# A two-layer encoder trunk on one core: two of the sums of Winograd's seven products merged into one VectorE operation, the up block split ahead of the gate block, one more pair on seven products, and the first unit's copies dealt out

## The chip, the core and the metric

The kernel runs on one core of a Trainium2 chip. TensorE (PE) multiplies, VectorE (DVE) and ScalarE (ACT) work on the vectors, GpSimd (POOL) does a few of them, and SP issues most transfers. The metric is the device time of one execution in microseconds. Before the change it is 1954.49 us, the median of three runs that lie between 1954.39 and 1954.78. The profiled execution took 1953.67 us, of which 1951.9 us lie between its first and its last instruction.

## What is computed

The input is 256 tokens of width 2048 in float32, with BATCH 1. There are two layers. In the first the token mixer is grouped-query attention (16 query heads, 4 key heads, head size 128), in the second a gated linear recurrence with a short convolution. After each mixer stands the same feed-forward part, with a hidden width of 5632:

```python
x = x + mix
x = x + swiglu(rms_norm(x, norm_ffn[i]), ffn_w_gate[i], ffn_w_up[i], ffn_w_down[i])

def swiglu(h, w_gate, w_up, w_down):
    return (jax.nn.silu(h @ w_gate) * (h @ w_up)) @ w_down
```

The change lies wholly in the feed-forward part, and there in `h @ w_gate` and `h @ w_up`. The two feed-forward parts are the stretches from about 265 to 950 us and from about 1260 us to the end.

## The kernel before

**Precision.** TensorE is fed a float32 number as a sum of two numbers of a shorter type (fp32r): hi is the value cast by ScalarE, lo is the value less hi, subtracted by VectorE. A product of two blocks is then three matmuls: hi by hi, lo by hi and hi by lo (`product`, L322 to L328). Every weight therefore passes ScalarE once (a cast) and VectorE once (a subtraction) before TensorE can use it.

**A unit.** The hidden width is worked off in 11 units of 512 features a layer, numbered 0 to 10 (`unit`, L765). In a unit the contraction over 2048 goes in eight pairs of 256 rows, numbered 0 to 7. For one pair the weights are a 2 by 2 arrangement of blocks of 128 by 512: b11 and b21 are the two row halves of the gate weights, b12 and b22 those of the up weights. The tokens are a 2 by 2 arrangement as well, with two row halves of the pair and two halves of the 256 tokens. A plain pair makes all eight block products, 24 matmuls. A pair on seven products (a "seven" below) forms sums of weights and of tokens first, in Winograd's way, and makes seven products, 21 matmuls. `SEVEN` names the pairs that do so, and `FEWER` the shorter lists of units 0, 1 and 2.

**The weights of a seven** (`load_seven`, L155 to L196). Two transfers of 512 KB on SP's queue bring the gate weights into raw[0] and the up weights into raw[1], each 128 by 1024. Then

- t1, the sum of b11 and b12, is formed in place of b12, by VectorE where the three loads before were plain (L175), and otherwise by a transfer that accumulates, issued by GpSimd (L177);
- raw[0] and raw[1] are split into hi and lo, 1024 wide (cast L164, subtraction L165);
- t2, t3 and t4 are formed one after another by three additions or subtractions 512 wide (L170), each cast by ScalarE (L171), and each given its lo (L172).

A plain pair takes two loads of 1024, each with one cast (L146) and one subtraction (L147).

**Order.** TensorE's instructions stand as written. Those of the other engines are placed by a scheduler, but two chains bind it: every cast of a weight follows the cast before it ("cast"), and every subtraction or sum of weights the one before it ("rest"), by `behind`, L125. An engine executes its instructions in the order in which they stand. hi and lo live in a ring of seven tiles, raw in a ring of eight, and t2 has two tiles of its own.

**The end of a unit.** VectorE adds the accumulators (`sums` L779 to L784, then L802 and L805), ScalarE applies SiLU, VectorE multiplies (L806) and transposes 32 by 32 blocks (L409), and 16 copies of 32 by 256 (L417) put these blocks in place. The hidden features are then split (cast L812, subtraction L813). Where `beside` is set, the copies are dealt out: four stand at each of the next four sevens, at the `tail.pop(0)()` of `load_seven`. Otherwise all 16 stand together. From unit 2 on, two groups of the down projection follow a unit (96 matmuls on plain weights), whose sums ScalarE scales (L829) and GpSimd adds to x by an accumulating transfer.

Of the kernel before, what the change touches and what calls it, by code (L numbers as in the profile page):

```python
# [27 lines left out]
PARTS = [8, 8, 8, 8, 12]  # L28
UNIT = 4
SEVEN = (0, 1, 2, 4, 5, 6)  # L30
FEWER = {0: (0, 5, 6), 1: (4, 5, 6), 2: (1, 4, 5, 6)}
HALF = 8
CHUNK = HALF * P
WIDE = 512
# [41 lines left out]
def trunk(ctx, tc, w, out):  # L76
# [48 lines left out]
    def behind(key, i):  # L125
        if key in newest:
            follow(i, newest[key])
        newest[key] = i
        for rule in [rule for rule in ahead if key == rule[2]]:
            rule[0] -= 1  # L130
            if rule[0] == 0:
                follow(i, rule[1])
                ahead.remove(rule)
# [21 lines left out]
    def load_seven(srcs, soon):  # L155
        raw = [landing([P, 2, WIDE]) for _ in range(2)]
        for r, src in zip(raw, srcs):
            sync.dma_start(out=r, in_=src)
        (b11, b21), (t1, b22) = ([r[:, j, :] for j in range(2)] for r in raw)
        got = {}  # L160

        def two(src, names):
            hi, lo = parts([P, 2, WIDE])
            behind("cast", act.copy(hi, src))  # L164
            behind("rest", dve.tensor_tensor(lo, src, hi[:].bitcast(F32), ALU.subtract))  # L165
            for j, name in enumerate(names):
                got[name] = hi[:, j, :], lo[:, j, :]

        def combine(o, x, y, op, hi, lo):
            behind("rest", dve.tensor_tensor(o, x, y, op))  # L170
            behind("cast", act.copy(hi, o))  # L171
            return lambda: behind("rest", dve.tensor_tensor(lo, o, hi.bitcast(F32), ALU.subtract))  # L172

        if soon:
            behind("rest", dve.tensor_tensor(t1, b11, t1, ALU.add))  # L175
        else:
            pool.dma_start(out=t1, in_=b11, accum_op=ALU.add)  # L177
        two(raw[0], ("b11", "b21"))
        two(raw[1], ("t1", "b22"))
        if tail:  # L180
            tail.pop(0)()
        one = [tmp(t, (P, WIDE), F32R) for t in ("ohi", "olo")]
        hi, lo = parts([P, 2, WIDE])
        got["t2"] = tuple(one)
        got["t3"], got["t4"] = ((hi[:, j, :], lo[:, j, :]) for j in range(2))
        t2 = b22
        rests = [
            combine(t2, t1, b22, ALU.add, *got["t2"]),
            combine(b11, t2, b11, ALU.subtract, *got["t3"]),
            combine(b21, t2, b21, ALU.add, *got["t4"]),  # L190
        ]
        while parted:
            follow(parted.pop(), newest["cast"])
        for rest in rests:
            rest()
        return got  # L196


# [226 lines left out]
    class Norm:  # L425
# [38 lines left out]
        def form(self, c, src):  # L464
            v, t = (tmp("form", (P, 2 * S)).rearrange("p (a b) -> p a b", a=n) for n in (2, 4))
            for j in range(2):
                act.activation(v[:, j, :], src[:, j, :], AF.Copy, scale=col(self.g[0], self.g[1] + 2 * c + j))
            (a11, a21), (a12, a22) = ([v[:, j, a * P : (a + 1) * P] for a in range(2)] for j in range(2))
            for i, x, y, op in (
                (0, a21, a22, ALU.subtract), (1, a11, a21, ALU.subtract),  # L470
                (2, t[:, 0, :], a11, ALU.subtract), (3, a12, t[:, 2, :], ALU.add),
            ):
                pool.tensor_tensor(t[:, i, :], x, y, op)
            hi, lo = (tmp(f"f{n}", (P, 4, P), F32R, bufs=len(SEVEN)) for n in "hl")
            act.copy(hi, t)
            dve.tensor_tensor(lo, t, hi[:].bitcast(F32), ALU.subtract)
            self.forms[c] = [(hi[:, i, :], lo[:, i, :]) for i in range(4)]
# [283 lines left out]
    def ffn(norm, nxt):  # L761
# [3 lines left out]
        def unit(seven, beside, engines, soon):  # L765
# [20 lines left out]
            for c in range(KT // 2):  # L786
                if c not in seven:
                    for pair in ((c11, c21), (c12, c22)):
                        wide(pair, xs, 2 * c, KT, [fresh(o) for o in pair])
                        if pair[0] is c11 and c == seven[-1] + 1:  # L790
                            sums()
                    continue
                wt, end = half(), c == seven[-1]
                n1, n3, n2, n4 = norm.forms[c]
                a11, a12, a22 = block(xs, 2 * c, 0), block(xs, 2 * c + 1, 0), block(xs, 2 * c + 1, 1)
                for o, y, b in (
                    (m1, a11, "b11"), (c11, a12, "b21"), (p5, n1, "t1"), (c12, n4, "b22"),
                    (p6, n2, "t2"), (p7, n3, "t3"), (c21, a22, "t4"),
                ):
                    product(o, y, wt[b], fresh(o), end and any(o is m for m in (m1, p5, p7, p6)))  # L800
# [21 lines left out]
        ends = np.cumsum(PARTS) // UNIT  # L822
        for what, i in ffn_plan():
            if what == "unit":
                hid[int(np.searchsorted(ends, i, "right"))] += unit(FEWER.get(i, SEVEN), 0 < i < ends[-1] - 1, (act,) if i < ends[-1] - 1 else (act, dve), i < ends[0])
            else:
                for a, acc in enumerate(wide_project(hid[i[0]], PARTS[i[0]], bank)):
                    t = tmp("form", (P, WIDE))
# [224 lines left out]
```

## Time and profile before

| | before |
|---|---|
| runs, us | 1954.39 to 1954.78, median 1954.49 |
| profiled execution, us | 1953.67, span 1951.9 |
| TensorE, ScalarE, VectorE, GpSimd busy | 99%, 74%, 91%, 21% |
| granted TensorE clock | 1.000 |
| from one unit's sums to the next, units 3 to 10 | 61.2 us |

In the profile, L12 is line 12 of the kernel. A row of the groups names the line, the engine, the operation, out<-in by the program's names without buffer numbers, the shape and the count; then the busy time and the mean duration of one, and the idle time of the engine just before. In a timeline the columns are start, duration, engine, line and operation; square brackets hold the idle time before the instruction and who ended it. Where several equal instructions stand in one row, the duration is that of all. Matmuls are pipelined: each is shown with about 0.39 us, but they start 0.2267 us apart, as the starts in the timeline show.

### The profile page before, as it was taken

The page shows a single profiled execution, that of the slowest core. Times are in us where ns is not written, and L with a number is a line of the kernel's source. Part 1 is how long each engine was busy: PE and PEld are TensorE (multiplying, and loading weights), DVE is VectorE, ACT ScalarE, POOL GpSimd, SP SyncE. Part 2 cuts the span into 40 slices and gives each one's busy share as a digit, 9 for nine tenths or more (in the row PEclk, how much of TensorE's full clock was granted, in tenths as well). Part 3 has the DMA queues.
Part 4 walks back from the last instruction along what each step waited for, and adds up shares of the span by engine and source line. Part 5 has one row for each costly group of instructions (what it writes and reads, how often), then busy time and mean ns, then how long its engine had stood idle before and what let it go on. Part 6 is the DMA issues. An engine that isn't in the chain of part 4 may idle for free.

```text
span 1951.9 us, 27724 instructions
## 1 busy us (share of the span) xinstructions
PE 1939.2 (99%) x9264; PEld 1626.1 (83%) x9264; DVE 1771.2 (91%) x2425; ACT 1450.3 (74%) x2366; POOL 403.0 (21%) x497
## 2 busy tenths in 40 slices
PE   9999999999999999999999999999999999999999
PEld 8898888788888888888899998887888888888887
DVE  7878698999999999998799997898999999999993
ACT  7677686777777777777699887866778776787772
POOL 0443250011101111010466450520101110011100
PEclk9999999999999999999999999999999999999999
DMA  8434746697878978787365556565878888788872
GB/s 320 157 127 152 248 157 201 197 270 238 249 232 242 261 243 246 233 243 248 127 218 192 189 164 246 173 200 171 250 236 246 247 247 255 228 245 255 244 258 86
DMA packets 131729, 426.44 MB, mean 218 GB/s; under 512 B 14721, under 2 KB 14977, under 8 KB 131585
## 3 DMA queue, kind: packets, MB, share of 16 engines
q1 hardware_dynamic: 108944, 383.21, 58.2%
q0 software_dynamic: 22496, 41.43, 11.9%
q8 instruction: 73, 1.20, 0.2%
q14 instruction: 72, 0.58, 0.1%
q10 hardware_dynamic: 144, 0.02, 0.0%
HBM read 382.13 MB, written 2.10 MB: 197 GB/s over the span
## 4 chain that ended last, share of the span: by engine, by line
PE 92%; DVE 5%; issue 1%; ACT 1%; DMA 1%; POOL 0%; SPq 0%; ACTq 0%; DVEq 0%; POOLq 0%
PE acc L327 14%; PE acc L324 14%; PE acc L325 14%; PE pm L327 11%; PE pm L325 11%; PE pm L324 11%; PE acc L295 9%; PE acc L293 5%; PE pm L307 1%; PE pm L308 1%; PE pm L306 1%; DVE lo L147 1%; DVE lo L165 1%; ACT hi L146 0%; DVE raw L170 0%
## 5 line engine op out<-in xcount | busy, mean ns | idle before, releaser
L147 DVE TENSOR_TENSOR lo<-raw,hi 128x1024 fp32r<-128x1024 f32 (+1 forms) x474 | 577.8, 1247 | 75.3 <-ACT hi L146 73.7
L146 ACT CAST hi<-raw 128x1024 fp32r<-128x1024 f32 (+1 forms) x474 | 478.7, 1045 | 111.2 <-PE acc L325 68.3
L295 PE MATMUL acc<-xg,hi 128*128 128x512 f32 x896 | 293.3, 398 | 0.3 <-DVE xg L437 0.3
L165 DVE TENSOR_TENSOR lo<-raw,hi 128x1024 fp32r<-128x1024 f32 x232 | 275.3, 1217 | 7.4 <-ACT hi L164 5.3
L327 PE MATMUL acc<-lo,xg 128*128 128x512 f32 x712 | 277.9, 390 | 2.0 <-DVE lo L147 2.0
L325 PE MATMUL acc<-hi,xg 128*128 128x512 f32 x712 | 277.1, 389 | 0.0
L324 PE MATMUL acc<-hi,xg 128*128 128x512 f32 x712 | 277.1, 389 | 0.0
L164 ACT CAST hi<-raw 128x1024 fp32r<-128x1024 f32 x232 | 235.0, 1049 | 42.5 <-issue 14.9
L177 POOL DMA_DIRECT2D raw<-raw x90 | 77.8, 865 | 899.3 <-DVE raw L175 307.1
L293 PEld LDWEIGHTS acc<-xg,lo 128*128 128x128 f32 x896 | 168.1, 188 | 37.6 <-DVE lo L147 2.6
L327 PE MATMUL pm<-lo,act 128*128 128x512 f32 x512 | 199.2, 389 | 0.0
L325 PE MATMUL pm<-hi,act 128*128 128x512 f32 x512 | 199.2, 389 | 0.0
L324 PE MATMUL pm<-hi,act 128*128 128x512 f32 x512 | 199.2, 389 | 0.0
L417 ACT COPY two<-one 32x256 f32<-32x256 f32 x420 | 169.7, 404 | 24.7 <-DVE one L409 16.5
L293 PE MATMUL acc<-xg,lo 128*128 128x256 f32 x896 | 185.5, 281 | 1.0 <-DVE lo L147 1.0
L324 PE MATMUL acc<-hi,act 128*128 128x512 f32 x448 | 174.9, 390 | 0.4 <-DVE two L805 0.4
L327 PE MATMUL acc<-lo,act 128*128 128x512 f32 x448 | 174.4, 389 | 0.0
L325 PE MATMUL acc<-hi,act 128*128 128x512 f32 x448 | 174.4, 389 | 0.0
L171 ACT CAST hi<-raw 128x512 fp32r<-128x512 f32 x232 | 137.2, 622 | 32.7 <-DVE raw L170 31.3
L327 PEld LDWEIGHTS acc<-lo,xg 128*128 128x128 f32 x712 | 133.6, 188 | 32.7 <-DVE lo L147 5.3
L325 PEld LDWEIGHTS acc<-hi,xg 128*128 128x128 f32 x712 | 133.7, 188 | 28.0
L324 PEld LDWEIGHTS acc<-hi,xg 128*128 128x128 f32 x712 | 133.7, 188 | 27.4
(223 smaller groups left out, 3869.2 us busy)
## 6 DMA issues: line engine op xcount, KB each, us to landing
raw<-in_w_gate_dram SPq DMA_DIRECT2D x176, 512.0 KB, 4.7
raw<-in_w_up_dram SPq DMA_DIRECT2D x176, 512.0 KB, 5.4
raw<-in_w_down_dram SPq DMA_DIRECT2D x176, 512.0 KB, 4.5
raw<-in_w_in_dram SPq DMA_DIRECT2D x64, 512.0 KB, 4.4
raw<-raw POOLq DMA_DIRECT2D x90, 256.0 KB, 6.0
raw<-in_w_qv_dram SPq DMA_DIRECT2D x40, 512.0 KB, 4.2
raw<-in_w_o_dram SPq DMA_DIRECT2D x32, 512.0 KB, 3.7
x<-form POOLq DMA_DIRECT2D x64, 256.0 KB, 6.7
```

The costliest lines, as they stand in the source:

```text
L146: behind("cast", act.copy(hi[:, sl], raw[:, sl]))
L147: behind("rest", dve.tensor_tensor(lo[:, sl], raw[:, sl], hi[:, sl].bitcast(F32), ALU.subtract))
L164: behind("cast", act.copy(hi, src))
L165: behind("rest", dve.tensor_tensor(lo, src, hi[:].bitcast(F32), ALU.subtract))
L171: behind("cast", act.copy(hi, o))
L177: pool.dma_start(out=t1, in_=b11, accum_op=ALU.add)
L293: pe.matmul(acc[:, S:], w, xs[k][:, :S], start=False, stop=stop)
L295: pe.matmul(acc, w, xs[k], start=(k == 0), stop=stop)
L324: pe.matmul(o, xh, wh, start=start, stop=False)
L325: pe.matmul(o, xl, wh, start=False, stop=False)
L327: pe.matmul(o, xh, wl, start=False, stop=stop)
L417: m = (eng.copy if eng is act else eng.tensor_copy)(to[:, :, :, i, :], of[:, :, :, j, :])
```

## The change

Four things are changed; the signs of some sums of tokens change with the weights' and cost nothing else.

1. In `load_seven` the up block, with t1, is split first, then the gate block. t2 is now t1 less b22. The third and fourth sums are b11 less t2 and b21 less t2, so that one operation makes both: raw[0] less t2, where t2 is read twice by a broadcast. They are cast by one operation 1024 wide and get their lo by one subtraction 1024 wide.
2. TensorE takes the products in another order: t1 and b22 first, then b11 and b21, then t2, t3 and t4 as before.
3. Unit 1 makes pair 2 as a seven too, and unit 2 has pair 2 in the place of pair 1.
4. Unit 0's copies are dealt out to unit 1's sevens, as was done for the other units.

```diff
-FEWER = {0: (0, 5, 6), 1: (4, 5, 6), 2: (1, 4, 5, 6)}
+FEWER = {0: (0, 5, 6), 1: (2, 4, 5, 6), 2: (2, 4, 5, 6)}
...
-        def combine(o, x, y, op, hi, lo):
-            behind("rest", dve.tensor_tensor(o, x, y, op))
-            behind("cast", act.copy(hi, o))
-            return lambda: behind("rest", dve.tensor_tensor(lo, o, hi.bitcast(F32), ALU.subtract))
-
         if soon:
             behind("rest", dve.tensor_tensor(t1, b11, t1, ALU.add))
         else:
             pool.dma_start(out=t1, in_=b11, accum_op=ALU.add)
+        two(raw[1], ("t1", "b22"))
+        hi, lo = one = [tmp(t, (P, WIDE), F32R) for t in ("ohi", "olo")]
+        behind("rest", dve.tensor_tensor(b22, t1, b22, ALU.subtract))
         two(raw[0], ("b11", "b21"))
-        two(raw[1], ("t1", "b22"))
+        behind("cast", act.copy(hi, b22))
         if tail:
             tail.pop(0)()
-        one = [tmp(t, (P, WIDE), F32R) for t in ("ohi", "olo")]
-        hi, lo = parts([P, 2, WIDE])
-        got["t2"] = tuple(one)
-        got["t3"], got["t4"] = ((hi[:, j, :], lo[:, j, :]) for j in range(2))
-        t2 = b22
-        rests = [
-            combine(t2, t1, b22, ALU.add, *got["t2"]),
-            combine(b11, t2, b11, ALU.subtract, *got["t3"]),
-            combine(b21, t2, b21, ALU.add, *got["t4"]),
-        ]
+        t2 = b22.unsqueeze(1).to_broadcast([P, 2, WIDE])
+        behind("rest", dve.tensor_tensor(raw[0], raw[0], t2, ALU.subtract))
+        both = parts([P, 2, WIDE])
+        behind("cast", act.copy(both[0], raw[0]))
         while parted:
             follow(parted.pop(), newest["cast"])
-        for rest in rests:
-            rest()
+        behind("rest", dve.tensor_tensor(lo, b22, hi[:].bitcast(F32), ALU.subtract))
+        behind("rest", dve.tensor_tensor(both[1], raw[0], both[0][:].bitcast(F32), ALU.subtract))
...
-                    (m1, a11, "b11"), (c11, a12, "b21"), (p5, n1, "t1"), (c12, n4, "b22"),
+                    (p5, n1, "t1"), (c12, n4, "b22"), (m1, a11, "b11"), (c11, a12, "b21"),
                     (p6, n2, "t2"), (p7, n3, "t3"), (c21, a22, "t4"),
...
-                hid[int(np.searchsorted(ends, i, "right"))] += unit(FEWER.get(i, SEVEN), 0 < i < ends[-1] - 1, (act,) if i < ends[-1] - 1 else (act, dve), i < ends[0])
+                hid[int(np.searchsorted(ends, i, "right"))] += unit(FEWER.get(i, SEVEN), i < ends[-1] - 1, (act,) if i < ends[-1] - 1 else (act, dve), i < ends[0])
```

What the change moves is seen best engine by engine. In the rows below a name stands with its buffer number, as in raw_5332; the changed kernel's lines behind `load_seven` have numbers lower by six.

VectorE, pair 5 of unit 4 in the first layer, before. raw_5332 is the gate block, raw_5333 the up block with t1:

```order
L165 TENSOR_TENSOR lo_5338<-raw_5332,hi_5337 128x1024
L165 TENSOR_TENSOR lo_5342<-raw_5333,hi_5341 128x1024
L170 TENSOR_TENSOR raw_5333<-raw_5333 128x512
L170 TENSOR_TENSOR raw_5332<-raw_5333,raw_5332 128x512 x2
L172 TENSOR_TENSOR olo_5346<-raw_5333,ohi_5345 128x512
L172 TENSOR_TENSOR lo_5348<-raw_5332,hi_5347 128x512 x2
```

The same pair with the change, where raw_5280 is the gate block and raw_5281 the up block:

```order
L165 TENSOR_TENSOR lo_5286<-raw_5281,hi_5285 128x1024
L175 TENSOR_TENSOR raw_5281<-raw_5281 128x512
L165 TENSOR_TENSOR lo_5293<-raw_5280,hi_5292 128x1024
L181 TENSOR_TENSOR raw_5280<-raw_5280,raw_5281 128x1024
L186 TENSOR_TENSOR olo_5290<-raw_5281,ohi_5289 128x512
L187 TENSOR_TENSOR lo_5299<-raw_5280,hi_5298 128x1024
```

Eight instructions are six now, and only one of 512 stands between the sum L181 and the subtraction L187, which needs the cast of that sum; before, three stood between the last sum and the subtraction of its cast.

ScalarE in unit 4, pair 1, before. The copies L417 belong to the unit before, the L829 to the down projection:

```order
L164 CAST hi_5146<-raw_5141 128x1024
L164 CAST hi_5150<-raw_5142 128x1024
L417 COPY two_4532<-one_4918 32x8x32 x4
L829 ACTIVATE form_5074<-pm_5000,nr_3227 128x512
L829 ACTIVATE form_5077<-pm_5001,nr_3227 128x512
L171 CAST ohi_5158<-raw_5142 128x512
L171 CAST hi_5160<-raw_5141 128x512 x2
```

With the change:

```order
L164 CAST hi_5103<-raw_5099 128x1024
L164 CAST hi_5110<-raw_5098 128x1024
L823 ACTIVATE form_5034<-pm_4960,nr_3227 128x512
L823 ACTIVATE form_5037<-pm_4961,nr_3227 128x512
L177 CAST ohi_5107<-raw_5099 128x512
L411 COPY two_4510<-one_4878 32x8x32 x4
L183 CAST hi_5120<-raw_5098 128x1024
```

The four copies have moved from ahead of t2's cast to behind it, and stand now ahead of the cast of the third and fourth sums.

ScalarE at the first seven of unit 1 in the first layer, pair 4 before:

```order
L164 CAST hi_3801<-raw_3796 128x1024
L164 CAST hi_3805<-raw_3797 128x1024
L417 COPY two_3287<-one_3622 32x8x32 x16
L171 CAST ohi_3809<-raw_3797 128x512
L171 CAST hi_3811<-raw_3796 128x512 x2
```

With the change, where the first seven of unit 1 is pair 2:

```order
L164 CAST hi_3702<-raw_3698 128x1024
L164 CAST hi_3709<-raw_3697 128x1024
L177 CAST ohi_3706<-raw_3698 128x512
L411 COPY two_3287<-one_3613 32x8x32 x4
L183 CAST hi_3719<-raw_3697 128x1024
```

Sixteen copies in a row are four, behind t2's cast instead of ahead of it; the other twelve stand in the same place of the next three sevens.

More of the change, by code (lines that the diff above doesn't have):

```diff
@@ L177, in load_seven @@
             pool.dma_start(out=t1, in_=b11, accum_op=ALU.add)
+        two(raw[1], ("t1", "b22"))
+        hi, lo = one = [tmp(t, (P, WIDE), F32R) for t in ("ohi", "olo")]
+        behind("rest", dve.tensor_tensor(b22, t1, b22, ALU.subtract))
         two(raw[0], ("b11", "b21"))
-        two(raw[1], ("t1", "b22"))
+        behind("cast", act.copy(hi, b22))
         if tail:
             tail.pop(0)()
-        one = [tmp(t, (P, WIDE), F32R) for t in ("ohi", "olo")]
-        hi, lo = parts([P, 2, WIDE])
-        got["t2"] = tuple(one)
-        got["t3"], got["t4"] = ((hi[:, j, :], lo[:, j, :]) for j in range(2))
-        t2 = b22
-        rests = [
-            combine(t2, t1, b22, ALU.add, *got["t2"]),
-            combine(b11, t2, b11, ALU.subtract, *got["t3"]),
-            combine(b21, t2, b21, ALU.add, *got["t4"]),
-        ]
+        t2 = b22.unsqueeze(1).to_broadcast([P, 2, WIDE])
+        behind("rest", dve.tensor_tensor(raw[0], raw[0], t2, ALU.subtract))
+        both = parts([P, 2, WIDE])
+        behind("cast", act.copy(both[0], raw[0]))
         while parted:
             follow(parted.pop(), newest["cast"])
-        for rest in rests:
-            rest()
+        behind("rest", dve.tensor_tensor(lo, b22, hi[:].bitcast(F32), ALU.subtract))
+        behind("rest", dve.tensor_tensor(both[1], raw[0], both[0][:].bitcast(F32), ALU.subtract))
+        got["t2"] = tuple(one)
+        got["t3"], got["t4"] = (tuple(t[:, j, :] for t in both) for j in range(2))
         return got
@@ L469, in form @@
             for i, x, y, op in (
-                (0, a21, a22, ALU.subtract), (1, a11, a21, ALU.subtract),
-                (2, t[:, 0, :], a11, ALU.subtract), (3, a12, t[:, 2, :], ALU.add),
+                (0, a21, a22, ALU.add), (1, a21, a11, ALU.subtract),
+                (2, t[:, 0, :], a11, ALU.subtract), (3, a12, t[:, 2, :], ALU.subtract),
             ):
```

## The prediction

> **What bounds the kernel now.** I read the page's busy times first, then the windows, then the timelines of one unit.
>
> ```profile
> span 1951.9 us, 27724 instructions
> PE 1939.2 (99%) x9264; PEld 1626.1 (83%) x9264; DVE 1771.2 (91%) x2425; ACT 1450.3 (74%) x2366; POOL 403.0 (21%) x497
> ```
>
> TensorE is the bound, at 99%. A change of the vector engines' work helps only where TensorE waits. Where that is, the windows of 40 us show (columns: TensorE, weight loads, VectorE, ScalarE, GpSimd busy, with counts; then clock, DMA share, GB/s). A full window in the feed-forward part has 178 matmuls, as the first row has; the other four are those with fewer:
>
> ```profile
> 440.00:480.00 40.00, 40.00 (x178) 33.14 (x177) 38.49 (x48) 28.92 (x42) 4.37 (x5) 1.00 0.77 241
> 320.00:360.00 40.00, 39.17 (x171) 31.49 (x170) 35.47 (x45) 25.79 (x43) 0.86 (x1) 1.00 0.56 171
> 360.00:400.00 40.00, 38.61 (x167) 30.84 (x166) 38.72 (x49) 34.60 (x50) 1.71 (x2) 1.00 0.69 221
> 1320.00:1360.00 40.00, 37.96 (x164) 29.96 (x163) 34.98 (x46) 26.91 (x44) 0.00 (x0) 1.00 0.45 144
> 1360.00:1400.00 40.00, 39.52 (x172) 31.73 (x171) 38.56 (x47) 31.93 (x45) 1.71 (x2) 1.00 0.75 238
> ```
>
> 38 matmuls are missing in these four, at 0.2267 us 8.6 us. All four lie in units 1 and 2. In the first layer the loss begins here:
>
> ```profile
> 321.83 6.63 ACT L417 COPY two<-one 32x256 f32<-32x256 f32 x16 [1.10 <-DVE one L409]
> 329.14 0.69 DVE L172 TENSOR_TENSOR olo<-raw,ohi 128x512 fp32r<-128x512 f32 x1 [4.18 <-ACT ohi L171]
> 352.28 0.50 PE L327 MATMUL acc<-lo,xg 128*128 128x512 f32 x1 [0.82 <-DVE lo L147]
> 361.50 0.50 PE L324 MATMUL pm<-ohi,fh 128*128 128x512 f32 x1 [1.22 <-ACT ohi L171]
> ```
>
> Sixteen copies hold t2's cast, VectorE idles 4.18 us, and TensorE waits at the end of unit 1 and in the first seven of unit 2.
>
> Everywhere else TensorE is full, but VectorE nearly is too. These two windows are two whole units of the steady part (units 4 and 5):
>
> ```profile
> 452.00:513.20 61.20, 61.20 (x272) 50.67 (x271) 59.25 (x73) 45.62 (x67) 7.84 (x9) 1.00 0.83 244
> 513.20:574.40 61.20, 61.20 (x272) 50.68 (x271) 59.25 (x73) 45.73 (x67) 7.84 (x9) 1.00 0.84 246
> ```
>
> VectorE works 59.25 of 61.20 us. How near it is to being late shows at the unit's last seven, pair 6: t3's and t4's lo are done at 508.58 + 1.28 = 509.86 us, and TensorE takes t3's at 511.32.
>
> ```profile
> 508.58 1.28 DVE L172 TENSOR_TENSOR lo<-raw,hi 128x512 fp32r<-128x512 f32 x2
> 511.32 0.39 PE L327 MATMUL pm<-lo,fh 128*128 128x512 f32 x1
> ```
>
> So VectorE may become 1.46 us later per unit before TensorE waits. That number decides this change.
>
> **One seven before and after.** Pair 5 of unit 4, VectorE then ScalarE:
>
> ```profile
> 497.52 2.35 DVE L165 TENSOR_TENSOR lo<-raw,hi 128x1024 fp32r<-128x1024 f32 x2
> 499.90 0.69 DVE L170 TENSOR_TENSOR raw<-raw 128x512 f32<-128x512 f32 x1
> 500.63 1.29 DVE L170 TENSOR_TENSOR raw<-raw,raw 128x512 f32<-128x512 f32 x2
> 501.84 0.69 DVE L172 TENSOR_TENSOR olo<-raw,ohi 128x512 fp32r<-128x512 f32 x1
> 502.44 1.29 DVE L172 TENSOR_TENSOR lo<-raw,hi 128x512 fp32r<-128x512 f32 x2
> 503.65 2.36 DVE L165 TENSOR_TENSOR lo<-raw,hi 128x1024 fp32r<-128x1024 f32 x2
> 500.63 0.62 ACT L171 CAST ohi<-raw 128x512 fp32r<-128x512 f32 x1 [2.28 <-DVE raw L170]
> 501.41 1.17 ACT L171 CAST hi<-raw 128x512 fp32r<-128x512 f32 x2 [0.16 <-DVE raw L170]
> L806 DVE TENSOR_TENSOR two<-two,one 128x1024 f32<-128x1024 f32 x22 | 26.8, 1216 | 0.0
> L164 ACT CAST hi<-raw 128x1024 fp32r<-128x1024 f32 x232 | 235.0, 1049 | 42.5 <-issue 14.9
> L417 ACT COPY two<-one 32x256 f32<-32x256 f32 x420 | 169.7, 404 | 24.7 <-DVE one L409 16.5
> ```
>
> A seven takes 503.65 - 497.52 = 6.13 us of VectorE, without idle time: an operation of 1024 follows another after 1.14 us, one of 512 after 0.60, and one that needs the result just before it starts 0.03 after that has ended. Casts never hold it up, since two sums and two subtractions lie between a sum and the subtraction of its cast. ScalarE starts 0.04 to 0.09 after the sum.
>
> With the change VectorE goes: lo of the up block 1.14; t2, which overwrites what was just read, 0.03 + 0.69 = 0.72; lo of the gate block 1.14; the merged sum L181, dependent on what was just read, 0.03 + 1.22 = 1.25 (duration of L806, also f32 in place; no row has a repeated operand). Then ScalarE has to cast that sum, 1024 wide: start after 0.06, 1.05 long, and 0.03 later lo of both starts, 1.22 long. VectorE has only t2's lo (0.60) to do in between, and `behind` lets no later pair's work ahead. Sum: 1.14 + 0.72 + 1.14 + 1.25 + 0.06 + 1.05 + 0.03 + 1.22 = **6.61 us, 0.48 more**. Without the wait of some 0.6 us it would be 5.99, that is 0.14 less.
>
> The Trainium skill, in "Perfetto Trace Analysis", Optimizing Scalar/DVE Operations, says that grouping into larger operations can improve throughput if the engine is saturated, at about 60 ns of overhead for each DVE operation. The saving agrees with the rows (twice 0.60 less 1.14 is 0.06), but by that rule alone the change would be faster, the first rival's time. The same section says that where vector engines cause bubbles on others, breaking instructions up may let work be completed sooner; by that the merged cast comes too late, as in my sum.
>
> **A steady unit (3 to 10).** The rows for its pairs 1 to 6:
>
> ```profile
> 478.47 0.69 ACT L829 ACTIVATE form<-pm,nr 128x512 f32<-128x512 f32 x1 [0.67 <-PE pm L327]
> 479.06 0.61 ACT L171 CAST ohi<-raw 128x512 fp32r<-128x512 f32 x1
> 479.70 0.69 DVE L172 TENSOR_TENSOR olo<-raw,ohi 128x512 fp32r<-128x512 f32 x1 [0.91 <-ACT ohi L171]
> 480.31 1.29 DVE L172 TENSOR_TENSOR lo<-raw,hi 128x512 fp32r<-128x512 f32 x2
> 486.63 1.28 DVE L172 TENSOR_TENSOR lo<-raw,hi 128x512 fp32r<-128x512 f32 x2
> 490.10 2.35 DVE L165 TENSOR_TENSOR lo<-raw,hi 128x1024 fp32r<-128x1024 f32 x2
> 496.31 1.29 DVE L172 TENSOR_TENSOR lo<-raw,hi 128x512 fp32r<-128x512 f32 x2
> ```
>
> Pair 1 is tied to TensorE: the second scaling L829 waits for the down projection's last matmul and starts at 478.47 in either kernel, and t2's cast stands behind it. Before, pair 1 ended at 481.60. Now follow t2's cast (to 479.67), the four copies that the order put there (4 x 0.404, to 481.3), the cast of both (1.05) and lo of both (0.03 + 1.22): 483.6, **2.0 later**. Pair 2 took 6.31 (481.60 to 487.91) and takes 6.61: +0.30. The plain pair 3 stays. Pair 4 contains the hidden features' lo (L813): 490.18 to 497.60, 7.42. Now that subtraction fills the wait for the cast: 1.14 + 0.72 + 0.04 to t2's cast, 0.61, copies 1.62, cast L812 1.05, cast of both 1.05, and lo 1.22 with two starts, 7.5: +0.07. Pairs 5 and 6 +0.48 each. Together 3.33 us late against a margin of 1.46: TensorE waits **1.87 us in each steady unit**. The next unit starts from TensorE's scalings again, so each pays anew: 8 units in each of 2 layers, 29.9 us. ScalarE has room: a seven costs it 1.05 x 3 + 0.62 and 1.62 of copies, 5.4 of 6.6.
>
> **Units 0 to 2.** Dealing the copies out removes the 4.18 us of idle time. But unit 1's pair 2 takes VectorE 6.61 instead of 2 x 1.14 = 2.28, +4.33, and saves TensorE three matmuls, 0.68 (in two layers 1.36). Unit 0's sevens, in which small work fills the wait, I leave alone; its base copy stands behind one more cast, about 1 us, of which TensorE waits 0.3. Counted on so, unit 1's pair 2 ends with next to nothing in hand (0.1). Pair 3 gives 24 x 0.2267 = 5.44 less 2.28, +3.16. The three sevens each cost 6.61 against TensorE's 21 x 0.2267 = 4.76, -5.55, and L813 -0.9: TensorE waits 3.2. The wait behind the unit's sums stays (1.1, with the 0.82 quoted). Unit 2 now starts with two plain pairs, so the 1.22 there goes; its pair 2 ends about 0.75 ahead: 0.75 + 3.16 - 5.55 - 0.9, TensorE waits 2.5. Sum 0.3 + 3.2 + 1.1 + 2.5 = 7.1 a layer, 14.2 for 8.6 before: +5.6.
>
> **Sum.** 29.9 + 5.6 - 1.36 = +34.1 us on the profiled execution's 1953.67: 1987.8. That execution lies 0.8 below the runs' median, so the median forecast is **1988.6 us**.
>
> **Bounds.** L181 with a repeated operand: from 0.60 (a 512 row, if reading half as much counted) to 1.25; I take 1.25, as L806 handles the same 1024 outputs. If t2 and L181 pay no wait for the operation before them, a seven takes 6.38, and the units pay about 1.0 instead of 1.87: 1972. With 0.60 for L181 it takes 5.96 and no unit stalls, near the first rival's time. A start of the cast 0.16 after the sum instead of 0.06 adds 0.4 a unit: 1995.
>
> **Rivals.** *Fewer operations win.* If the wait for the cast is filled or short, VectorE saves 0.14 a seven and the 0.91 of pair 1, every wait of units 1 and 2 goes, and what is left is 1954.5 - 1.4 - 8.6 = 1944.5. For it: the 8.6 us are real, and the copies are dealt out. Against: VectorE's row order leaves one operation of 0.60 between L181 and L187. It decides if a seven costs less than about 6.0. *A draw.* The steady units absorb the delay, if it stays below 1.46 us a unit, and units 1 and 2 trade one wait for another: 1954 +- 4. *The accumulated t1 is late.* The up block is now split first, so ScalarE needs t1 a cast earlier:
>
> ```profile
> 487.94 0.33 SPq L158 DMA_DIRECT2D raw<-in_w_up_dram  x1
> 494.84 0.86 POOL L177 DMA_DIRECT2D raw<-raw  x1 [5.57 <-DVE act L813]
> raw<-raw POOLq DMA_DIRECT2D x90, 256.0 KB, 6.0
> ```
>
> From the freed buffer of pair 2 to t1 of pair 6 these are 6.9 + 6.0 = 12.9 us; from pair 2's end (490.2) to the need (505.4) there are 15.2. It decides when the two transfers take over 15.2; at 1.2 us late on three pairs a unit it costs 16 x 1.2 more: 2008.
>
> **Chances.** The forecast 0.74; draw 0.08, half of it still slower; fewer operations 0.10; late t1 0.08. The range 1966 to 2002 holds the forecast with its bounds and part of the third rival's. A measurement here can tell about 0.2%, 4 us, from no change: faster 0.10, same 0.04, slower 0.86.
>
> **What would show it.** Right: in the rows of the changed kernel, L187 waiting for L183 about 0.5 us in most of its 118 instances (some 50 us in all), a steady unit of about 63.1 us, and TensorE waiting at the last seven of each unit; no idle of 4 us in unit 1. Wrong: a steady unit of 61.2 us, or a pair's L165 following the pair before's by 6.1 us or less.

## The result and the profile after

The changed kernel takes 2004.67 us (median of four runs, 2003.53 to 2005.99) against 1954.61 for the kernel before: a ratio of 1.0257, with a 95% interval of 1.0244 to 1.0270. The forecast was 1988.6 in a range of 1966 to 2002. Direction and mechanism are as forecast; the size is 16 us short, and the time lies above the range. The profiled execution took 2003.53 us, 49.9 more than that of before.

The page's busy times of the changed kernel:

```profile
span 2001.7 us, 27361 instructions
PE 1964.3 (98%) x9258; PEld 1620.3 (81%) x9258; DVE 1768.2 (88%) x2199; ACT 1433.8 (72%) x2254; POOL 410.2 (20%) x501
```

VectorE has 226 instructions fewer and 3.0 us less work, ScalarE 16.5 us less. TensorE shows 25 us more although it has six matmuls fewer; it can't have more to do, so its busy time holds part of its delay (a matmul behind a wait is drawn with 0.50 us instead of 0.39, and the one ahead of it keeps its 0.39 although 0.2267 is its share). So busy times don't say what happened; the chain that ended last does. Its shares, of the changed kernel and then of the kernel before:

```profile
PE 63%; DVE 18%; ACT 9%; issue 7%; DMA 1%; POOL 1%; DVEq 0%; SPq 0%; ACTq 0%; POOLq 0%
```

```profile
PE 92%; DVE 5%; issue 1%; ACT 1%; DMA 1%; POOL 0%; SPq 0%; ACTq 0%; DVEq 0%; POOLq 0%
```

The chain now runs through VectorE and ScalarE. Where, the waits of the changed kernel tell (engine, line and what it waited for; us in total, times, longest):

```profile
DVE lo L187 <- ACT hi L183: 71.7, 96, 2.1
PE pm L321 <- DVE lo L187: 16.4, 39, 0.7
PE pm L321 <- DVE olo L186: 3.8, 19, 0.2
```

VectorE waits 71.7 us for the cast of the merged sum. TensorE waits for the lo of the merged sum ("lo of both" below, L187) and, less, for t2's lo (L186). Pairs 5 and 6 of unit 4 in the changed kernel, VectorE:

```profile
506.45 1.22 DVE L165 TENSOR_TENSOR lo<-raw,hi 128x1024 fp32r<-128x1024 f32 x1
507.70 0.69 DVE L175 TENSOR_TENSOR raw<-raw 128x512 f32<-128x512 f32 x1
508.31 1.22 DVE L165 TENSOR_TENSOR lo<-raw,hi 128x1024 fp32r<-128x1024 f32 x1
509.57 1.23 DVE L181 TENSOR_TENSOR raw<-raw,raw 128x1024 f32<-128x1024 f32 x1
510.71 0.69 DVE L186 TENSOR_TENSOR olo<-raw,ohi 128x512 fp32r<-128x512 f32 x1
511.97 1.23 DVE L187 TENSOR_TENSOR lo<-raw,hi 128x1024 fp32r<-128x1024 f32 x1 [0.57 <-ACT hi L183]
513.11 1.22 DVE L165 TENSOR_TENSOR lo<-raw,hi 128x1024 fp32r<-128x1024 f32 x1
518.57 1.23 DVE L187 TENSOR_TENSOR lo<-raw,hi 128x1024 fp32r<-128x1024 f32 x1 [0.51 <-ACT hi L183]
```

From one pair's L187 to the next these are 6.60 us, where a seven took 6.13; 0.51 is the wait. And TensorE at the end of that unit:

```profile
513.25 0.50 PE L321 MATMUL pm<-lo,fh 128*128 128x512 f32 x1 [0.21 <-DVE lo L187]
518.11 0.49 PE L321 MATMUL pm<-olo,fh 128*128 128x512 f32 x1 [0.20 <-DVE olo L186]
519.85 0.50 PE L321 MATMUL pm<-lo,fh 128*128 128x512 f32 x1 [0.53 <-DVE lo L187]
520.18 0.40 PE L318 MATMUL acc<-hi,xg 128*128 128x512 f32 x1
```

Three waits stand where the kernel before had none, and the matmul after a wait starts 0.33 us behind it (519.85 to 520.18), not 0.2267. The losses add up from the start of each unit's first matmul in both profiles, since the matmuls between two such starts are the same in number but for the three that unit 1 saves:

| stage, both layers together | forecast, us | measured, us |
|---|---|---|
| units 3 to 10 (16 units) | +29.9 (1.87 each) | +38.6 (2.34 in most) |
| units 0 to 2, with six matmuls fewer | +4.2 | +9.9 (4.35 and 5.60) |
| behind unit 10's sums | 0 | +1.5 |
| all else (attention, recurrence, start) | 0 | -0.1 |

### The profile page after: what moved, and what is told of

Same layout as the page of the kernel before. It is cut to its first block, busy times and chain, and to the rows that moved or that the text cites. A ratio compares the mean times of both kernels' runs of the same rounds, so it can differ in the third digit from the quotient of the medians.

```text
span 2001.7 us, 27361 instructions
## 1 busy us (share of the span) xinstructions
PE 1964.3 (98%) x9258; PEld 1620.3 (81%) x9258; DVE 1768.2 (88%) x2199; ACT 1433.8 (72%) x2254; POOL 410.2 (20%) x501
## 4 chain that ended last, share of the span: by engine, by line
PE 63%; DVE 18%; ACT 9%; issue 7%; DMA 1%; POOL 1%; DVEq 0%; SPq 0%; ACTq 0%; POOLq 0%
PE acc L318 9%; PE acc L321 9%; PE acc L319 9%; PE acc L289 9%; DVE lo L165 7%; PE pm L321 7%; PE pm L319 6%; PE pm L318 6%; PE acc L287 4%; ACT hi L183 3%; DVE raw L181 3%; DVE lo L147 3%; ACT two L411 2%; DVE lo L187 2%; PE pm L301 1%
## 5 line engine op out<-in xcount | busy, mean ns | idle before, releaser
L147 DVE TENSOR_TENSOR lo<-raw,hi 128x1024 fp32r<-128x1024 f32 (+1 forms) x470 | 573.6, 1248 | 73.0 <-ACT hi L146 71.7
L165 DVE TENSOR_TENSOR lo<-raw,hi 128x1024 fp32r<-128x1024 f32 x236 | 288.6, 1223 | 2.1 <-ACT hi L164 1.6
L321 PE MATMUL acc<-lo,xg 128*128 128x512 f32 x700 | 273.8, 391 | 2.9 <-DVE lo L147 2.9
L318 PE MATMUL acc<-hi,xg 128*128 128x512 f32 x700 | 273.8, 391 | 1.0 <-DVE one L796 1.0
L319 PE MATMUL acc<-hi,xg 128*128 128x512 f32 x700 | 273.2, 390 | 0.0
L164 ACT CAST hi<-raw 128x1024 fp32r<-128x1024 f32 x236 | 235.7, 1047 | 26.7 <-DVE raw L170 16.9
L187 DVE TENSOR_TENSOR lo<-raw,hi 128x1024 fp32r<-128x1024 f32 x118 | 144.6, 1225 | 71.8 <-ACT hi L183 71.7
L183 ACT CAST hi<-raw 128x1024 fp32r<-128x1024 f32 x118 | 123.9, 1050 | 69.2 <-DVE raw L181 67.7
L177 ACT CAST ohi<-raw 128x512 fp32r<-128x512 f32 x118 | 73.2, 620 | 134.9 <-DVE raw L175 117.6
```

What stands on the lines that cost most here:

```text
L147: behind("rest", dve.tensor_tensor(lo[:, sl], raw[:, sl], hi[:, sl].bitcast(F32), ALU.subtract))
L183: behind("cast", act.copy(both[0], raw[0]))
L187: behind("rest", dve.tensor_tensor(both[1], raw[0], both[0][:].bitcast(F32), ALU.subtract))
L318: pe.matmul(o, xh, wh, start=start, stop=False)
L319: pe.matmul(o, xl, wh, start=False, stop=False)
L321: pe.matmul(o, xh, wl, start=False, stop=stop)
```

## The experiments

All kernels but new_split_old_units have the new lists of sevens and unit 0's copies dealt out. "Lost per steady unit" is the median, over units 3 to 9 of both layers, of a unit's length by the matmuls' starts less 61.20, the kernel before's.

| kernel | median, us | ratio to before (95%) | lost per steady unit, us |
|---|---|---|---|
| changed | 2004.67 | 1.0244 to 1.0270 | 2.34 |
| new_split_old_units | 2006.71 | 1.0251 to 1.0284 | 2.39 |
| old_split_new_units | 1954.39 | 0.9992 to 1.0011 | 0.00 |
| t2_lo_first | 2037.70 | 1.0408 to 1.0445 | 3.96 |
| copies_ahead | 1992.65 | 1.0178 to 1.0214 | 1.39 |
| halves | 1994.45 | 1.0188 to 1.0220 | 1.87 |
| both_mended | 1978.24 | 1.0107 to 1.0139 | 0.90 |
| sums_apart | 1978.1 | 1.0099 to 1.0135 | 0.95 (in its profile) |
| apart_copies_ahead | 1953.10 | 0.9984 to 1.0003 | 0.00 |
| merged_gate_first | 1983.68 | 1.0134 to 1.0164 | 1.15 |
| skewed | 2008.64 | 1.0262 to 1.0295 | 3.22 |
| skewed_sevens | 2028.81 | 1.0363 to 1.0397 | 4.09 |
| skewed_gate | 1958.40 | 1.0011 to 1.0029 | 0.00 |
| skewed_gate_all | 1955.66 | 0.9996 to 1.0014 | 0.00 |

**The two halves of the change apart.** First load_seven and the order of products alone:

```diff
-FEWER = {0: (0, 5, 6), 1: (2, 4, 5, 6), 2: (2, 4, 5, 6)}
+FEWER = {0: (0, 5, 6), 1: (4, 5, 6), 2: (1, 4, 5, 6)}
...
-unit(FEWER.get(i, SEVEN), i < ends[-1] - 1,
+unit(FEWER.get(i, SEVEN), 0 < i < ends[-1] - 1,
```

> The change's load_seven and order of products (parts 1 and 2) with the lists of sevens and the bunched copies of before. Theory (the wait for the merged cast makes each seven longer): the steady units stay at 63.5 us from sums to sums, as in the changed kernel, 2.34 x 16 = 37 us; units 0 to 2 and the stall after unit 10 add a few us: 1992 to 2000. Rival (dealing out unit 0's copies and the new lists cost much of the 50 us, by what they push into the later units): steady units below 62.3 us and a time under 1980.

Measured 2006.71, above the expected 1992 to 2000; the steady units lose 2.39 us, as in the changed kernel (2.34), and units 0 to 2 lose 13.6 where the changed kernel loses 9.9. Then the lists and the dealt-out copies alone, on the kernel before:

> The new lists of sevens and the dealt-out copies (parts 3 and 4) with load_seven and the order of products of before. Theory: sevens stay at 6.13 us and steady units at 61.2; counted as in the prediction with 6.13 in the place of 6.61, units 0 to 2 lose some 3 us a layer where they lost 4, and six matmuls fewer save 1.36: 1951, between 1946 and 1953. Rival (the units' part costs something of its own): 1958 or more, since the changed kernel's early units lose 19 us in both layers.

Measured 1954.39, no change, against a forecast of 1951 (1946 to 1953). Its profile shows 2.7 us gained in units 0 to 2 (1.36 of it the six matmuls), and 4.6 lost in the recurrence between the layers, most of it at one place:

```profile
1008.21 0.47 PE L295 MATMUL acc<-xg,hi 128*128 128x512 f32 x1 [2.15 <-DVE act L382]
```

This wait makes 2.5 us. Behind it the granted TensorE clock was 0.50 (1010 to 1012 us; 0.79 and 0.85 in the 2 us before and after), and that makes 1.6 more. The edit doesn't touch this code, but the scheduler set other engines' work there in another order. That profiled execution was the longest of ten: the four with a mean clock of 1.000 took 1953.49 to 1954.12 us, the six with 0.998 or 0.999 1953.72 to 1955.64. How much of the wait itself the others have is left open. What is settled: parts 3 and 4 cost next to nothing and cannot be the 50 us; these come with parts 1 and 2.

**More of the wait.** t2's lo is moved ahead of the merged sum, so that nothing fills the wait for its cast:

```diff
+        behind("rest", dve.tensor_tensor(lo, b22, hi[:].bitcast(F32), ALU.subtract))
         t2 = b22.unsqueeze(1).to_broadcast([P, 2, WIDE])
         behind("rest", dve.tensor_tensor(raw[0], raw[0], t2, ALU.subtract))
...
-        behind("rest", dve.tensor_tensor(lo, b22, hi[:].bitcast(F32), ALU.subtract))
         behind("rest", dve.tensor_tensor(both[1], raw[0], both[0][:].bitcast(F32), ALU.subtract))
```

> The changed kernel, but t2's lo stands ahead of the merged sum, so that nothing is left between that sum and the subtraction that needs its cast. Theory (the wait for the cast of the merged sum sets the length of a seven): the wait grows by the 0.60 us that t2's lo no longer fills, pairs 2, 5 and 6 go from 6.6 to 7.2 us, and a steady unit, where pair 1 is held by ScalarE's copies anyway, loses 1.8 to 2.4 more: 16 x 2.1 = 34 us and some 8 in units 0 to 2, about 2045 (2030 to 2055). Rival (the amount of work counts, not its order): the same work, 2005.

Measured 2037.7, in the expected range, with a steady unit 1.6 us longer than in the changed kernel (1.8 to 2.4 expected): the work is the same, the order makes 33 us. The wait of the seven that ends at 520 us is 1.17 where it was 0.57:

```profile
517.55 1.22 DVE L182 TENSOR_TENSOR raw<-raw,raw 128x1024 f32<-128x1024 f32 x1
519.94 1.23 DVE L187 TENSOR_TENSOR lo<-raw,hi 128x1024 fp32r<-128x1024 f32 x1 [1.17 <-ACT hi L184]
```

**The copies' place.** The copies stand ahead of t2's cast again:

```diff
-        behind("cast", act.copy(hi, b22))
         if tail:
             tail.pop(0)()
+        behind("cast", act.copy(hi, b22))
```

> The changed kernel, but the four copies stand ahead of t2's cast again, as before the change. Theory (of pair 1's 2.06 us, 1.62 are the copies between t2's cast and the merged cast): pair 1 is only some 0.45 late, but the hidden features' lo no longer fills the wait of pair 4, +0.3 there; a steady unit is 3.6 - 1.6 + 0.3 = 2.3 late against 1.46 of margin, so it loses 0.8 to 1.0 where it lost 2.3: about 1980 (1972 to 1985). Rival (the copies' place does not matter, only the six waits): 2000 or more.

Measured 1992.65, above the expected 1972 to 1985: a unit still loses 1.39. In units 4 and 5 of this kernel VectorE waits for the merged cast in all six sevens of a unit, pair 4 included (0.54 us each), and for nothing else. Its 58.95 us of work a unit, these waits and the short starts behind an operation's own input fill the 62.7 us of the unit, so no margin is left that could swallow a delay.

**The merged cast and lo in halves**, the merged sum kept:

```diff
-        behind("cast", act.copy(both[0], raw[0]))
+        for j in range(2):
+            behind("cast", act.copy(both[0][:, j, :], raw[0][:, j, :]))
...
-        behind("rest", dve.tensor_tensor(both[1], raw[0], both[0][:].bitcast(F32), ALU.subtract))
+        for j in range(2):
+            behind("rest", dve.tensor_tensor(both[1][:, j, :], raw[0][:, j, :], both[0][:, j, :].bitcast(F32), ALU.subtract))
```

> The changed kernel, but the merged sum is cast and given its lo in two halves of 512 (the sum itself stays one operation of 1024). Theory (what costs is that VectorE waits for a cast of 1024): t3's cast of 0.62 ends while t2's lo of 0.60 runs, so the wait in a seven falls from 0.6 to about 0.1 and a seven to 6.2 us; pair 1, whose copies still stand behind t2's cast, stays 1.6 late, so a steady unit loses some 0.3 and the time is about 1960 (1953 to 1968). Rival (the other order of the two blocks costs, not the wait): 1995 or more.

Measured 1994.45, against the 1960 of the theory and close to the rival's 1995. The rival falls further down, with sums_apart and the copies ahead. The wait inside a seven did fall, but a seven became hardly shorter (pair 5 takes 505.49 to 512.05 us, that is 6.56). Pair 5 of unit 4 in this kernel, VectorE and then ScalarE:

```profile
508.61 1.23 DVE L181 TENSOR_TENSOR raw<-raw,raw 128x1024 f32<-128x1024 f32 x1
509.75 0.69 DVE L187 TENSOR_TENSOR olo<-raw,ohi 128x512 fp32r<-128x512 f32 x1
510.57 1.29 DVE L189 TENSOR_TENSOR lo<-raw,hi 128x512 fp32r<-128x512 f32 x2
512.05 1.23 DVE L165 TENSOR_TENSOR lo<-raw,hi 128x1024 fp32r<-128x1024 f32 x1 [0.18 <-ACT hi L164]
```

```profile
509.92 1.14 ACT L184 CAST hi<-raw 128x512 fp32r<-128x512 f32 x2 [1.83 <-DVE raw L181]
510.97 2.00 ACT L164 CAST hi<-raw 128x1024 fp32r<-128x1024 f32 x2
```

VectorE now waits 0.18 us for the cast of the next pair's first block, which stands behind the two casts of this one. ScalarE had been idle for 1.83 us, until the merged sum was done. So the cycle is: merged sum, 1.05 us of casts for it, one more cast of about 1 us for the next block, and only then can VectorE's next pair begin. The theory had looked for the wait inside the seven alone. With both edits:

> The changed kernel with the merged sum's cast and lo in two halves, and the copies ahead of t2's cast. Halves alone took a steady unit's loss from 2.34 to 1.87 us, the copies alone to 1.39. Theory A (the delays of the pairs add up against one margin): 1.39 - 0.47 = 0.9 is left, and units 0 to 2 as with the copies ahead, 1985. Theory B (pair by pair: pair 1 level, pair 2 +0.25, pair 4 +0.3, pairs 5 and 6 +0.43 each, 1.4 against a margin of 1.46): hardly any loss in the steady units, 1960 to 1970.

Measured 1978.24, and 0.90 us lost in a steady unit: theory A to the digit, though the whole is 7 us better, by units 0 to 2.

**No merging.** Two sums of 512, with their casts and lo as in halves; the up block still comes first:

```diff
-        t2 = b22.unsqueeze(1).to_broadcast([P, 2, WIDE])
-        behind("rest", dve.tensor_tensor(raw[0], raw[0], t2, ALU.subtract))
+        for b in (b11, b21):
+            behind("rest", dve.tensor_tensor(b, b, b22, ALU.subtract))
```

> The changed kernel (up block first, copies behind t2's cast), but the third and fourth sums are two operations of 512 again, each with a cast and a lo of 512. It takes away the merging and leaves the other order of the blocks. Theory (merging is what makes VectorE and ScalarE wait for each other): a seven takes 6.12 us, only pair 1 stays late, by the copies, 1.6 against 1.46, and a steady unit loses 0.1 to 0.4: about 1961 (1954 to 1968). Rival (the order of the blocks costs by itself, since the third sum now waits for the gate block): a steady unit loses 1.5 or more, 1985 to 1995.

> The same kernel as sums_apart (two sums of 512, up block first, copies behind t2's cast), for a profile of it. If only the merged cast made sevens longer, pairs 5 and 6 take 6.1 to 6.2 us here and the units' loss, about 1 us by the time of 1978, is that of pair 1 alone; if the order of the blocks lengthens a seven too, pairs 5 and 6 take 6.4 us or more.

Measured 1978.1, between the theory and its rival; the profile (1977.05) has pair 5 at 6.13 us again. Late is pair 1 above all, and there by ScalarE's copies. ScalarE, then VectorE:

```profile
481.59 0.69 ACT L825 ACTIVATE form<-pm,nr 128x512 f32<-128x512 f32 x1 [0.67 <-PE pm L323]
482.17 0.61 ACT L177 CAST ohi<-raw 128x512 fp32r<-128x512 f32 x1
482.81 1.65 ACT L413 COPY two<-one 32x256 f32<-32x256 f32 x4
484.49 1.14 ACT L184 CAST hi<-raw 128x512 fp32r<-128x512 f32 x2
```

```profile
485.14 1.29 DVE L189 TENSOR_TENSOR lo<-raw,hi 128x512 fp32r<-128x512 f32 x2 [1.43 <-ACT hi L184]
```

Pair 1 ends 486.43 - 481.59 = 4.84 us after the second scaling starts, which was 3.13 before: 1.71 late; pairs 2 and 3 add 0.47, pair 4 0.22, pairs 5 and 6 nothing. 2.40 less the margin of 1.46 is 0.94, and the loss is 0.95. That agreement is luck in part: 1.46 is the margin of a lo of both in one, while here TensorE takes t3's lo without a wait, waits ahead of it for t2's lo (0.27 us), and starts the plain pair's first lo behind it 0.15 us late. Taking the copies away from there as well leaves only the order of the blocks:

> sums_apart, and the four copies ahead of t2's cast again: of the change's load_seven only the order of the two blocks is left, with the new units. Theory (the copies between t2's cast and the next casts are what is left of the loss in sums_apart): the 0.9 us a unit that moving them gained in the other two kernels comes off again, 16 x 0.9 = 15, so 1978 - 15 = 1963 (1957 to 1967). Rival (up block first costs by itself): 1970 or more.

Measured 1953.10, below the expected 1957 to 1967 and level with the kernel before: 25 us for one line's place, and up block first costs nothing in this form. The table of both places, with the three forms of the sums (us lost per steady unit):

| | copies ahead of t2's cast | behind it |
|---|---|---|
| sums, casts and lo apart | 0.00 | 0.95 |
| sum merged, casts and lo apart | 0.90 | 1.87 |
| all merged, as in the change | 1.39 | 2.34 |

Each row loses 0.95 to 0.97 more from left to right, each column 0.90 to 0.92 more by the merged sum and 0.47 to 0.49 by the merged cast and lo. The steady losses add up to within 0.02. One common margin would not make them do so: it should swallow 1.46 us of whichever delay comes first. In the kernels with the copies ahead the second scaling no longer waits for TensorE (in copies_ahead both scalings stand without idle time). In copies_ahead, where VectorE waits for ScalarE alone, the two run in a cycle of their own:

```profile
486.59 1.27 ACT L823 ACTIVATE form<-pm,nr 128x512 f32<-128x512 f32 x2
```

Why the losses add up so exactly stays open. Merging with the old order of blocks:

> The changed kernel's merged sum, cast and lo, but the gate block is split first, as before the change, with the products in that order and the copies ahead of t2's cast; the units are the new ones. Theory (merging alone costs): a seven takes the same 6.6 us by the same sum, so it loses as the kernel with the copies ahead did, 1.4 us a unit: 1985 to 1997. Rival (up block first is half of the loss): a steady unit loses 0.7 or less, under 1975.

Measured 1983.68, just under the theory's 1985 to 1997, and 1.15 us lost in a unit: merging costs in either order, 9 us less with the gate block first than in copies_ahead.

**Merging with the wait filled.** load_seven is cut in two, and the next pair's up block is cast and subtracted, and its t2 formed, between the merged sum and lo of both:

```diff
+        begin(n + 1)
         both = parts([P, 2, WIDE])
         behind("cast", act.copy(both[0], raw[0]))
```

> The changed kernel's merged operations, but the next pair's up block (or the next plain pair's first load) is cast and subtracted, and its t2 formed, between the merged sum and the subtraction that needs its cast; the copies stand ahead of t2's cast. Theory (the merged operations are cheaper by 0.14 us a seven, and only the wait cost): VectorE no longer waits for L183's counterpart (under 5 us in all), a seven takes about 6.0 us, steady units go back to 61.2: 1946 to 1956. Rival (a pair's last weights, subtracted 1.9 us later, are late for TensorE): steady units of 62.5 us or more, over 1975.

Measured 2008.64, where the theory had 1946 to 1956. A seven took the 6.0 us expected, but ScalarE waited elsewhere, for the accumulated t1:

```profile
ACT hi L159 <- DMA raw<-raw: 39.5, 17, 4.5
```

The changed kernel's waits have no such row. Here the up block is wanted earlier, by what now runs ahead, and at pair 4 its transfer stood behind GpSimd's two transfers to x, which wait for the scalings:

```profile
483.50 1.75 POOL L844 DMA_DIRECT2D x<-form  x2 [9.08 <-ACT form L841]
484.62 1.52 POOL L173 DMA_DIRECT2D raw<-raw  x1
```

Without begin for the plain pairs:

> As skewed, but only a next seven is begun early, a plain pair no more, so that pair 4's accumulating transfer no longer stands behind the x sums in GpSimd's queue and the base copy no longer behind one more cast. Theory (these two side effects, 1.45 and 1.46 us of VectorE's waits a unit, ate the gain of the skew): pairs 1 and 5 take 6.0 us, pairs 2 and 6 still wait 0.5, a steady unit is back at 61.2 to 61.6: 1952 to 1965. Rival (lo of both comes too late because a lo of 1024 now stands ahead of it): steady units of 62.5 us or more, over 1975.

Measured 2028.81, where the theory had 1952 to 1965, with 4.09 us lost in a unit: pairs 2 and 6 have their 0.52 us waits back, and casts of the up block still wait for t1's transfer (18.0 us, 11 times). Of the 20 us that it is worse than skewed, some 7 are the clock: in its profile TensorE's matmuls start 0.43 us apart in six stretches of about 3 us, each behind 1.8 to 1.9 us of waits, which costs 8.9 us, and in that of skewed in one (1.6 us). The mean granted clock was 0.995 in all four executions, and 0.999 to 1.000 in those of skewed. The other 13 us stay open. In the next kernel the next seven's gate block, which waits for no accumulation, fills the gap (begin splits raw[0]; the products stand in the order of before):

> The merged sum, cast and lo, with the gate block first (products in the order of before, copies ahead of t2's cast), and the next seven's gate block cast and subtracted between the merged sum and lo of both. A gate block does not wait for the accumulated t1, which made the skewed kernels late. Theory (the wait for the merged cast is the price of merging, and work that is ready fills it): pairs 1 and 5 take 6.0 us, pairs 2 and 6 wait 0.5, together some 0.8 late in a unit against 1.46, so steady units are back at 61.2: 1950 to 1957. Rival (a tile more of the ring in use, or lo of both 1.14 later, makes TensorE wait): steady units of 62 us or more, over 1967.

Measured 1958.40, 0.2% above the kernel before and just above the expected 1957. The steady units are back at 61.20. One seven of this kernel, VectorE, where L160 is a split, L195 the merged sum, L203 lo of both:

```profile
501.43 1.22 DVE L160 TENSOR_TENSOR lo<-raw,hi 128x1024 fp32r<-128x1024 f32 x1
502.68 0.69 DVE L191 TENSOR_TENSOR raw<-raw 128x512 f32<-128x512 f32 x1
503.40 1.23 DVE L195 TENSOR_TENSOR raw<-raw,raw 128x1024 f32<-128x1024 f32 x1
504.55 0.68 DVE L196 TENSOR_TENSOR olo<-raw,ohi 128x512 fp32r<-128x512 f32 x1
505.15 1.22 DVE L160 TENSOR_TENSOR lo<-raw,hi 128x1024 fp32r<-128x1024 f32 x1
506.28 1.22 DVE L203 TENSOR_TENSOR lo<-raw,hi 128x1024 fp32r<-128x1024 f32 x1
507.42 1.22 DVE L160 TENSOR_TENSOR lo<-raw,hi 128x1024 fp32r<-128x1024 f32 x1
```

This seven takes 5.99 us with no idle time, the prediction's figure without the wait. The window of that unit (columns as in the prediction's windows):

```profile
452.00:513.20 61.20, 61.20 (x272) 50.67 (x271) 58.41 (x61) 44.63 (x61) 7.80 (x9) 1.00 0.83 245
```

VectorE has 58.41 us to do where it had 59.25: six times 0.14, really saved, and worth nothing, because TensorE fills the unit. The last step gives the plain pairs the same treatment:

> As skewed_gate, but before a plain pair, too, its first load is cast and subtracted between the merged sum and lo of both. Theory (what skewed_gate still loses, some 7 us in units 0 to 2 and after unit 10, comes from the 0.52 us waits of the last seven in pairs 2 and 6): L187's counterpart hardly waits any more, units 0 to 2 lose 2 to 4 us less, steady units stay at 61.2: 1952 to 1956, level with the kernel before. Rival (the last seven's lo of both, which TensorE waits for there, now stands behind a lo of 1024 and comes 0.6 later): units 0 to 2 lose more than in skewed_gate, 1960 to 1964.

Measured 1955.66, as expected level with the kernel before (0.9996 to 1.0014). So merging need not cost the wait; but none of the kernels beats the one before by what can be told from no change.

## Why the prediction was right, and where it was wrong

The mechanism was forecast, and the runs show it: merging makes VectorE wait for ScalarE's cast, and TensorE then waits at a unit's last seven. What failed are the sizes of two terms of the sum: the loss in a steady unit (1.87 us forecast, 2.34 measured) and the loss in units 0 to 2 (4.2 us in both layers, 9.9 measured). A third term, behind unit 10, was put at nothing without a reason (1.5 measured).

*The seven of 6.61 us.* Right: 6.60, the merged sum 1.22 to 1.23 us long (1.22 taken), the waits 0.51 to 0.57 (more only in pair 1, by the copies, and in pair 0, so that the 50 us forecast in all are 71.7, in 96 of the 118 instances). In the kernel before, two operations of 512 stand between a sum and the subtraction of its cast: two sums for t2, a sum and a subtraction for t3, two subtractions for t4. The three named with the order of VectorE above are one too many. That the wait and not the work is the price is shown by t2_lo_first from one side and skewed_gate from the other. The Trainium skill's sentence on breaking instructions up ("Perfetto Trace Analysis", Optimizing Scalar/DVE Operations), which it gives for vector engines that aren't saturated but cause bubbles on others, is the one that held in this kernel, where TensorE was the bound. The one on grouping, given for a saturated engine, did not: apart 1953.10, merged 1992.65, all else equal.

*The steady unit of 1.87 us.* This is the term that failed first: it measured 2.34, so the forecast was 8.7 us too little in 16 units. Pair 1 ends 489.99 - 484.80 = 5.19 us after the second scaling starts, in these rows of VectorE and ScalarE:

```profile
488.77 1.22 DVE L187 TENSOR_TENSOR lo<-raw,hi 128x1024 fp32r<-128x1024 f32 x1 [1.37 <-ACT hi L183]
```

```profile
484.80 0.69 ACT L823 ACTIVATE form<-pm,nr 128x512 f32<-128x512 f32 x1 [0.67 <-PE pm L321]
```

It was 3.13, so pair 1 is 2.06 late (2.0 forecast). Pair 2 is 0.31 late (0.30), pairs 5 and 6 0.53 and 0.47 (0.48 each), and pair 4 0.25 where the forecast had 0.07. There lo of both was to follow its own cast. But the hidden features' lo stands ahead of it on VectorE and waits 0.45 us for a cast of its own, behind the copies, and lo of both starts 1.14 us after it:

```profile
504.18 1.22 DVE L807 TENSOR_TENSOR act<-two,act 128x1024 fp32r<-128x1024 f32 x1 [0.45 <-ACT act L806]
505.32 1.22 DVE L187 TENSOR_TENSOR lo<-raw,hi 128x1024 fp32r<-128x1024 f32 x1
```

That makes 3.62 where the forecast had 3.33. Less the margin of 1.46 it is 2.16. The rest, 0.18, lies for the most part in the margin, which took TensorE to start at once and to go on at its usual pace. TensorE starts 0.05 us after lo of both has ended (518.57 + 1.23 = 519.80, start at 519.85), and its next matmul comes 0.33 us later instead of 0.2267, which is 0.11 more. The two earlier waits in the unit hardly add to it, since TensorE still waits 0.53 us at the last one.

*Units 0 to 2.* The forecast had TensorE lose 7.1 us a layer; by the starts it is 9.1 and 11.0 (4.1 and 4.8 lost before, 4.35 and 5.60 by which these units became longer, and 0.68 for three matmuls fewer). The sevens' part came near (in the first layer some 4.5 us around unit 1's end and 3 around unit 2's, forecast 4.3 and 2.5). The small terms did not, above all the base copy (ScalarE's copy of an accumulator, L774, with which a unit's sums begin), which stands one cast later: forecast 0.3 us of TensorE's time, measured some 1.4 in the first layer. VectorE there, behind unit 0:

```profile
305.04 0.69 DVE L775 TENSOR_TENSOR one<-one,pm 128x512 f32<-128x512 f32 x1 [1.73 <-ACT one L774]
```

TensorE in the first layer (310.35) and in the second:

```profile
310.35 0.51 PE L321 MATMUL acc<-lo,xg 128*128 128x512 f32 x1 [0.94 <-DVE lo L147]
1331.07 0.47 PE L318 MATMUL acc<-hi,xg 128*128 128x512 f32 x1 [0.96 <-DVE one L796]
1332.71 0.74 PE L321 MATMUL acc<-lo,xg 128*128 128x512 f32 x1 [0.94 <-DVE lo L147]
1333.67 0.63 PE L319 MATMUL acc<-hi,xg 128*128 128x512 f32 x1
1334.10 0.63 PE L321 MATMUL acc<-lo,xg 128*128 128x512 f32 x1
```

In the second layer unit 0's sums, which free the accumulators for unit 1, are late as well. Behind the two waits the granted TensorE clock was 0.50 (1334 to 1336 us): eight matmuls from 1332.71 on start 0.43 us apart and take 3.5 us where they took 1.8, so 1.6 to 1.7 us of this layer's loss are the clock's. The forecast had no such term. Two of the four executions have a mean clock of 0.999 and two of 1.000, so not all need have it. That the idle 4.18 us in unit 1 would go was right. That dealing it out and the other list would pay was hardly so: 2.7 us on the old load_seven, 3.7 on the new one (new_split_old_units loses 13.6 in units 0 to 2, the changed kernel 9.9), 1.36 of either for the matmuls.

*Behind unit 10.* Not foreseen: its sums now come late for the down projection, 0.73 us a layer.

```profile
909.90 0.50 PE L318 MATMUL acc<-hi,act 128*128 128x512 f32 x1 [0.95 <-DVE two L799]
```

*The rivals.* "Fewer operations win" fell, and not only by the wait: with it filled, the time is 1955.66 and not 1944.5, since units 0 to 2 trade one wait for another (they are 1.5 us longer than before, with six matmuls fewer). "A draw" fell in the change, and is what apart_copies_ahead and skewed_gate_all do. A late t1 plays no part in the change, but does where the up block is wanted earlier (skewed).

*The range.* It took its bounds from the price of single operations, and these came out as taken. It had no bound for pair 4, the margin, the small terms of units 0 to 2 and the stretch behind unit 10, and these made the 16 us.

## What to carry to other kernels

Before two operations are merged, look at what the other engine does with the result: merging here saved 0.14 us of VectorE a seven, and let ScalarE start its casts only after the whole sum of 1024 instead of after the first 512, in a loop in which each engine waits for the other once per pair. Follow the whole loop to the next pair's first operation: shortening one wait of it (halves) only showed the next. And a saving on an engine that is near its limit, but is not the limit, is worth nothing, while its delay is paid in full as soon as the margin is used up.

## What was not expected of the hardware

An operand that is repeated by a broadcast costs nothing and saves nothing: L181 takes 1.22 to 1.23 us for 128 by 1024 in float32, as the subtractions of two full operands do. The matmul behind one that waited starts 0.33 us after it instead of 0.2267.

The granted clock fell to half where TensorE had stood still for 1.3 to 2.3 us within a few microseconds, and matmuls then started 0.43 us apart for about 3 us: once in the changed kernel's feed-forward parts, twice in copies_ahead, six times in skewed_sevens. It did not fall each time: in the changed kernel 1.85 us of waits before 348 us left the clock at 1.00.
